# A hybrid decoder layer on one core: the p projection for all tokens in the router, w_in split one step ahead, earlier row norms, later group norms

## The chip, the core and the metric

The kernel runs on one core of one Trainium2 chip. The metric is the device time of one execution in microseconds (us); lower is better. TensorE is called PE, its weight loads PEld, VectorE DVE, ScalarE ACT, GpSimd POOL and SyncE SP. SP only issues DMAs here; POOL issues the indirect ones, and both take their instructions strictly in order.

## The reference, cut to what is computed

One layer over 1024 tokens of width 1024: a Mamba-2 SSD mixer, a mixture of 64 experts (group top-1 of 8 groups, then expert top-2 of 8), and a gated embedding p (1024 x 256) that is projected and added.

```python
h = x + ssd_mixer(rms_norm(x), w_in, conv_w, ..., gnorm, w_out)
h = h + hier_moe(rms_norm(h), w_rg, w_re, w_gate, w_up, w_down)
gate = sigmoid(rms_norm(h) @ ple_w_gate + ple_b_gate)
h = h + gate * (p @ ple_w_proj)            # p: 1024x256, ple_w_proj: 256x1024
return rms_norm(h)
```

The mixer projects u = rms_norm(x) with w_in (1024 x 5152) into z, x, B, C and dt, runs a short convolution, scans 8 chunks of 128 tokens, normalises each of 4 groups of 512 channels and projects back with w_out.

## The kernel before

**SSD.** `ssd` works in two halves of 512 tokens (`hf`) and, in each, four groups (`g`): eight units. A unit's `project` makes ten tiles of 128 output columns: B and C, four of x, four of z. A tile is 24 matmuls (`mm3`, L204 to L206): weights and activations are each split into a high and a low part (`split`, L69 on ACT for wh, L70 on DVE for wl), and three products are summed over 8 blocks of the width. `proj` splits a tile's weights directly ahead of the tile's matmuls. Between the tiles, at step t, `plan` inserts the scan of the unit before (`front`, `back`), and of the unit before that the group norm (`norm`, at t = 0: L394 sums the squares over partitions, then a row of small DVE operations) and its application (`store`, at t = 2: L402 turns it, DVE scales yz, SP stores yn). `x_half(hf)` loads four tiles of x, squares them for the row norms, makes rs (L66), turns it (L177), loads x transposed, scales it and splits it into xh and xl. For the second half it runs inside the fourth unit, at t = 3 to 7. Its x tiles share the buffers "ac" (three) and "ec" (two) with the scan.

**Router.** `out_router` multiplies by w_out in three passes of 2, 3 and 3 token tiles; `route` then yields `first`, `second` and `third`, which for the last pass have no products to run beside (`for f in side: f()`). `first` and `second` are chains of small DVE operations; `third` ranks tokens (L688 and its neighbours on PE), builds one-hot rows (L706 on DVE), packs the token numbers (L714), makes row indices (`index`) and fetches the first group's rows from DRAM (`fetch`, L827); then it packs the gates (L714 again). Meanwhile the first 12 half-tiles (1 MB each) of expert weights are loaded by SP (`half`, L782).

**Experts.** `moe` runs 8 groups of 4 pairs of experts. PE order is written by hand. Each step (`up`, `down`, L1027) uses two halves of 1 MB; a ring of 8 such halves is refilled by SP as PE frees them. The PLE of group g (`ple`) is spread over the steps of group g + 1: turn h (L898), 32 gate products (L908), and per set of rows the projection of p: `turn_p` (2 transposes, L855, ACT copy L856) and `project_p` (4 matmuls of 128x512 over two halves, L861). p rows come by an indirect DMA of 128 rows x 256 (`fetch_p`, L827, after step 10). There are nine such sets: groups 0 to 5 inside groups 1 to 6, groups 6 and 7 early at the end of group 6 (`project`, L1109), and the second row set inside group 7. The tensors' names: w is a raw weight tile, XT the group's tokens turned, py, pup, pgate, pq and pc are PSUM tiles, ha and hb rows of h, uh and ul the two parts of a group's normalised rows, S its selection matrix.

**Order.** On all engines except where PE is ordered by hand, a scheduler sets the order from the program and its own expectations, so the written step numbers move more than their own instructions.

Of the kernel before, what the change touches and what calls it, by code (L numbers as in the profile page):

```python
# [20 lines left out]
KD = D // 128  # L21
# [20 lines left out]
class K:  # L42
# [64 lines left out]
    def ssd(self, left, right):  # L107
# [35 lines left out]
        def x_half(hf):  # L143

            ss, rs, *tmp = (wk.tile([128, HC], F32, name=n) for n in ("rs", "rs", "nt0", "nt1", "nt2"))
            cols = []

            def columns():
                for j in range(2):
                    w = wraw.tile([128, KD, 256], F32, name="w").rearrange("p a b -> p (a b)")  # L150
                    w = w.rearrange("p (k t) -> p k t", t=HT)
                    nc.sync.dma_start(w, a["xT"].rearrange("(k p) t -> p k t", p=128)[:, 4 * j:4 * j + 4,
                                                                                      hf * HT:(hf + 1) * HT])
                    cols.extend(w[:, k] for k in range(4))

            for i in range(HC):
# [3 lines left out]
                if i == HC - 1:  # L160
                    if hf == 0:
                        W.append(load(2 * DI, 2 * DI + 512))
                    columns()
# [14 lines left out]
            rsb = wk.tile([128, HT], F32, name="dT", bufs=1)  # L178
            nc.scalar.activation(rsb, pr.rearrange("p c t -> p (c t)"), AF.Copy)

            def scale(k):
                nc.vector.tensor_mul(cols[k], cols[k], rsb)
# [4 lines left out]
            yield  # L187
# [75 lines left out]
        def proj(w, i, x):  # L263
            wh = wsp.tile([128, KD, 128], F32R, name="wh")
            wl = wsp.tile([128, KD, 128], F32R, name="wl")
            self.split(wh, wl, w[:, :, i * 128:(i + 1) * 128])
            ps = self.ps_mm.tile([128, 512], F32, name="mm")
            mm3(ps, wh, wl, x)
            return ps

        def conv_tile(hf, w, i, x, m):
# [5 lines left out]
            ps = proj(w, i, x)  # L277
# [11 lines left out]
        def project(hf, g):  # L289
            x = X[hf]  # L290
            w = W.pop() if W else load(2 * DI + g * 128, 2 * DI + 512 + g * 128)
            xT, zT = [], zp.tile([128, 4, HT], F32, name="z")
            bT = conv_tile(hf, w, 0, x, 16 + g)
            yield
            cT = conv_tile(hf, w, 1, x, 20 + g)
            U[hf, g] = bT, cT, xT, zT
            yield
            for j in range(2):
                w = load(DI + g * 512 + j * 256)
                for i in range(2):  # L300
                    xT.append(conv_tile(hf, w, i, x, 4 * g + 2 * j + i))
                    yield
            for j in range(2):
                w = load(g * 512 + j * 256)
                for i in range(2):
                    nc.scalar.activation(zT[:, 2 * j + i], proj(w, i, x), AF.Silu)
                    yield
# [104 lines left out]
        X, SZ, U, W = {}, {}, {}, []  # L412
        for i, _ in enumerate(x_half(0)):
            if i == 0:
                nc.sync.dma_start(gk, a["ssd_norm_kp"])
            if i == HC - 1:
                small_loads()
# [3 lines left out]
        for hf, g in units:  # L421
# [35 lines left out]
    def out_router(self, st, tail, after_tail):  # L457
# [18 lines left out]
        self.gdd = dp.tile([128, 8, NE], F32, name="gdd")  # L476
        macc = self.macc
# [82 lines left out]
        for f in side:  # L560
            f()
# [21 lines left out]
    def route(self, t0, hs, rp, pr_p, wr, rb, macc):  # L583
# [95 lines left out]
        def third():  # L679
# [3 lines left out]
            for i in range(n + 1):  # L683
# [5 lines left out]
                if t0:  # L689
                    nc.tensor.matmul(pa[:, i], lhsT=self.onesb, rhs=macc, start=False, stop=True)  # L690
            adj, was = tl("adj", 8)[:, 0], self.more
# [29 lines left out]
            pack(self.mid, omi)  # L721
            started = tc.issue_after(self.index(rp).ins) if t0 + n == T // 128 else nullcontext()
# [16 lines left out]
    def moe_weights(self, st):  # L739
# [3 lines left out]
        wpp = cp.tile([128, 2, D], F32, name="wpp")  # L743
# [4 lines left out]
        self.pl = (wpg, wpp, bg, fn, mgp)  # L748

        def loads():  # L750
# [6 lines left out]
            for k in range(2):  # L757
                nc.sync.dma_start(wpp[:, k], a["ple_w_proj"][k * 128:(k + 1) * 128])
                yield
# [3 lines left out]
            for _ in range(10):  # L763
                yield
# [29 lines left out]
    def moe_buffers(self, st, ring):  # L794
# [4 lines left out]
        self.p0, self.po = (hp.tile([128, PD], F32, name=f"p{i}") for i in range(2))  # L799
# [39 lines left out]
    def fetch_p(self, g):  # L839
        if g < NGR - 1:  # L840
            self.gather(self.p0, self.a["p"], g)
        if self.first_of(g + 1) or g == NGR - 1:
            self.gather(self.po, self.a["p"], NGR + SET[g])
# [8 lines left out]
    def turn_p(self, p, pT, pc_):  # L852
        pt = pc_.tile([128, 2, 128], F32, name="pc")
        for k in range(2):
            self.nc.tensor.transpose(pt[:, k], p[:, k * 128:(k + 1) * 128], self.ident)  # L855
        self.nc.scalar.activation(pT, pt, AF.Copy)  # L856

    def project_p(self, pT, hf, pc_):
        pq = pc_.tile([128, 512], F32, name="pc")
        for k in range(2):  # L860
            self.nc.tensor.matmul(pq, lhsT=pT[:, k], rhs=self.pl[1][:, k, hf * 512:hf * 512 + 512],  # L861
                                  start=(k == 0), stop=(k == 1))
        return pq

    def ple(self, h, p, store, wk, pq_, pc_, own=(), pr=None):
# [3 lines left out]
        wpg, wpp, bg, fn, mgp = self.pl  # L869
# [23 lines left out]
        def tr(k0):  # L893
# [6 lines left out]
            if k0 and pr is None:  # L900
                self.turn_p(p, new("pT", [128, 2, 128]), pc_)
# [26 lines left out]
    def moe(self, s2, ring, sa):  # L928
        nc, tc, a = self.nc, self.tc, self.a
        mgp = self.pl[4]  # L930
# [5 lines left out]
        part = {"vT": vx[:, 0:1024].rearrange("p (k t) -> p k t", k=KD), "gt": vx[:, 1024:1536],  # L936
                "pT": vx[:, 1536:1792].rearrange("p (k t) -> p k t", k=2)}
# [164 lines left out]
        def ple_of(G, i, own=part):  # L1102
# [3 lines left out]
                bounds_check=T - 1, oob_is_err=False), wk, ps1, ps2, own,  # L1106
                            None if i else G.pr)

        def project(p, o):  # L1109

            self.turn_p(p, part["pT"], ps2)
            for hf in range(2):
                nc.scalar.activation(o[:, hf * 512:hf * 512 + 512], self.project_p(part["pT"], hf, ps2), AF.Copy)
                yield

        def ending(G):
# [3 lines left out]
            wpg, wpp, bg, fn, _ = self.pl  # L1120
# [138 lines left out]
        with tc.manual_schedule(engines={mybir.EngineType.PE}):  # L1259
            for g in range(NGR):  # L1260
# [20 lines left out]
                if g == NGR - 2:  # L1281
                    nxt.pr, cur.pr = self.h0[(g + 2) % 3], self.ho[(SET[g] - 1) % 3]
                    fill[2].append(lambda: self.gather(vx[:, 1792:], a["p"], g + 1))
                    early = [project(vx[:, 1792:], nxt.pr), project(self.p0, cur.pr)]
                    for n, x in ((17, 0), (18, 0), (20, 1), (21, 1)):
                        fill.setdefault(n, []).append(lambda x=x: next(early[x]))
# [172 lines left out]
```

## Time and profile before

| | us |
|---|---|
| median of 3 runs | 1950.36 (1946.88 to 1954.07) |
| the profiled execution's own time | 1954.31 |
| its span from the first to the last instruction | 1952.4 |
| SSD stage, about | 0 to 636 |
| w_out and router, about | 636 to 882 |
| experts and PLE, about | 882 to 1952 |

A timeline row gives start, duration, engine, line, output<-input, tile shape and, in brackets, the engine's idle time just before and what ended it. A waits row gives who waited for whom: total us, times, longest. An fp32 matmul (L861, L908) stands in the trace as two records; so the 36 products of L861 are x72.

### The profile page before, as it was taken

How to read it: one execution, taken by the hardware profiler on the slowest of the kernel's cores; microseconds unless marked ns; L12 is line 12 of the kernel's file. 1: busy time of each engine (PE TensorE's matmuls, PEld its weight loads, DVE VectorE, ACT ScalarE, POOL GpSimd, SP SyncE). 2: the span in 40 equal slices, each digit the busy share in tenths (PEclk: the TensorE clock that was granted, in tenths of full speed). 3: DMA queues.
4: the chain of work that ended last, by engine and by line, in shares of the span. 5: the costliest groups of instructions: out<-in, count | busy, mean ns of one | idle time of the engine just before them, and what ended most of it. 6: DMA issues, size and time to landing. Idle time of an engine off the chain costs nothing.

```text
span 1952.4 us, 23158 instructions
## 1 busy us (share of the span) xinstructions
PE 1848.3 (95%) x8702; PEld 1047.1 (54%) x8702; DVE 1031.5 (53%) x2194; ACT 749.5 (38%) x1040; POOL 182.7 (9%) x276
## 2 busy tenths in 40 slices
PE   6999997999999999979999999999999999999996
PEld 4778775777887678863343333433433334334334
DVE  5497896858988876573341514423325244143223
ACT  5476766557767533322021211312222113122223
POOL 1011110201111031021000000000000000000004
PEclk9999998999999999988999999999999999999998
DMA  7425444345442787956999999999999999998883
GB/s 220 118 75 137 115 134 127 88 97 134 110 110 53 243 294 238 346 195 254 422 421 394 401 421 385 412 412 383 420 382 404 420 373 423 404 375 325 337 322 109
DMA packets 192166, 538.39 MB, mean 276 GB/s; under 512 B 16046, under 2 KB 128688, under 8 KB 143920
## 3 DMA queue, kind: packets, MB, share of 16 engines
q1 hardware_dynamic: 177744, 514.21, 72.0%
q10 hardware_dynamic: 11008, 12.94, 2.0%
q0 software_dynamic: 3296, 9.70, 1.3%
q8 instruction: 70, 1.15, 0.2%
q14 instruction: 48, 0.39, 0.1%
HBM read 520.95 MB, written 17.69 MB: 276 GB/s over the span
## 4 chain that ended last, share of the span: by engine, by line
PE 81%; DMA 7%; DVE 7%; ACT 2%; issue 2%; POOL 1%; SPq 0%; POOLq 0%; ACTq 0%; DVEq 0%
PE pup L1027 11%; PE pgate L1027 11%; PE py L1027 10%; PE mm L206 6%; PE mm L204 6%; PE mm L205 6%; PE pq L908 6%; PE pc L1017 3%; PE mm L505 2%; PE mm L506 2%; PE mm L507 2%; DMA w<-in_w_up_dram 2%; PE pc L861 2%; DMA ac<-acd 2%; PE pc L1090 2%
## 5 line engine op out<-in xcount | busy, mean ns | idle before, releaser
L204 PE MATMUL mm<-xh,wh 128*128 128x512 f32 x640 | 265.6, 415 | 3.3 <-ACT xh L197 2.2
L206 PE MATMUL mm<-xh,wl 128*128 128x512 f32 x640 | 254.5, 400 | 8.4 <-DVE wl L70 8.3
L205 PE MATMUL mm<-xl,wh 128*128 128x512 f32 x640 | 253.9, 397 | 0.3 <-DVE xl L198 0.3
L1027 PE MATMUL pup<-w,XT 128*64 128x512 f32 x1016 | 239.1, 598 | 1.6 <-DMA w<-in_w_up_dram 1.6
L1027 PE MATMUL pgate<-w,XT 128*64 128x512 f32 x1000 | 232.7, 599 | 0.0
L1027 PE MATMUL py<-w,hT 128*64 128x512 f32 (+1 forms) x1024 | 227.1, 586 | 2.1 <-DMA w<-in_w_down_dram 2.1
L70 DVE TENSOR_TENSOR yx<-py,yx 128x512 fp32r<-128x512 f32 (+1 forms) x68 | 44.8, 659 | 234.2 <-ACT yx L69 234.2
L1027 PEld LDWEIGHTS py<-w,hT 128*64 128x64 f32 x1024 | 70.0, 137 | 146.2 <-issue 138.2
L1027 PEld LDWEIGHTS pup<-w,XT 128*64 128x64 f32 x1016 | 72.1, 136 | 141.9 <-issue 131.5
L206 PEld LDWEIGHTS mm<-xh,wl 128*128 128x128 f32 x640 | 122.6, 192 | 38.5 <-DVE wl L70 12.2
L204 PEld LDWEIGHTS mm<-xh,wh 128*128 128x128 f32 x640 | 122.9, 192 | 34.2 <-issue 4.5
L1027 PEld LDWEIGHTS pgate<-w,XT 128*64 128x64 f32 x1000 | 68.7, 137 | 134.2 <-issue 129.6
L205 PEld LDWEIGHTS mm<-xl,wh 128*128 128x128 f32 x640 | 123.0, 192 | 29.9 <-issue 4.3
L908 PE MATMUL pq<-wpg,vx 128*128 128x512 f32 x256 | 123.1, 607 | 0.0
L70 DVE TENSOR_TENSOR wl<-w,wh 128x1024 fp32r<-128x1024 f32 x80 | 97.4, 1220 | 46.4 <-ACT wh L69 46.4
L69 ACT ACTIVATE wh<-w 128x1024 fp32r<-128x1024 f32 x80 | 84.3, 1054 | 72.0 <-PE mm L205 59.4
L284 DVE SCALAR_TENSOR_TENSOR xbc<-raw,convw,xbc 128x512 f32<-128x512 f32 x144 | 109.7, 762 | 3.8 <-ACT xbc L282 2.7
L506 PE MATMUL mm<-wl,yh 128*128 128x512 f32 x256 | 99.3, 398 | 2.0 <-DVE wl L517 1.9
L505 PE MATMUL mm<-wh,yh 128*128 128x512 f32 x256 | 96.0, 402 | 4.8 <-ACT yh L69 4.6
L69 ACT ACTIVATE yx<-py 128x512 fp32r<-128x512 f32 (+1 forms) x68 | 38.9, 572 | 159.4 <-PE py L1027 159.4
L1058 ACT ACTIVATE hT<-pt 128x512 f32<-128x512 f32 x31 | 18.4, 593 | 211.5 <-PE pt L1056 211.5
L507 PE MATMUL mm<-wh,yl 128*128 128x512 f32 x256 | 98.0, 393 | 0.0
(360 smaller groups left out, 2815.6 us busy)
## 6 DMA issues: line engine op xcount, KB each, us to landing
w<-in_w_up_dram SPq DMA_DIRECT2D x127, 1024.0 KB, 9.5
w<-in_w_gate_dram SPq DMA_DIRECT2D x125, 1024.0 KB, 9.1
w<-in_w_down_dram SPq DMA_DIRECT2D x120, 1024.0 KB, 9.5
w<-in_w_in_dram SPq DMA_DIRECT2D x32, 1024.0 KB, 5.6
w<-in_w_out_dram SPq DMA_DIRECT2D x48, 512.0 KB, 5.2
ac<-acd SPq DMA_DIRECT2D x32, 512.0 KB, 9.3
w<-in_w_in_dram SPq DMA_DIRECT2D x16, 512.0 KB, 8.7
yn<-yz SPq DMA_DIRECT2D x32, 256.0 KB, 4.4
```

The source lines that it names most:

```text
L69: self.nc.scalar.activation(dst_h, src, AF.Copy)
L70: self.nc.vector.tensor_sub(dst_l, src, r_(dst_h))
L204: nc.tensor.matmul(ps, lhsT=wh[:, k], rhs=x[0][:, k], start=(k == 0), stop=False)
L205: nc.tensor.matmul(ps, lhsT=wh[:, k], rhs=x[1][:, k], start=False, stop=False)
L206: nc.tensor.matmul(ps, lhsT=wl[:, k], rhs=x[0][:, k], start=False, stop=(k == KD - 1))
L284: nc.vector.scalar_tensor_tensor(o, raw[:, j:j + HT], convw[:, m, j:j + 1], o, op0=OP.mult, op1=OP.add)
L505: nc.tensor.matmul(po[i][hf], lhsT=yh[:, ts], rhs=wh[:, cs], start=(k == 0), stop=False)
L506: nc.tensor.matmul(po[i][hf], lhsT=yh[:, ts], rhs=wl[:, cs], start=False, stop=False)
L507: nc.tensor.matmul(po[i][hf], lhsT=yl[:, ts], rhs=wh[:, cs], start=False, stop=(k == 15))
L908: nc.tensor.matmul(V["pq"], lhsT=V["vT"][:, k], rhs=wpg[:, k, cs], start=(k == 0), stop=(k == KD - 1))
L1017: nc.tensor.matmul(px, lhsT=x[:, k], rhs=G.S[:, i], start=(i == 0 and x is u[i][0]), stop=(i == 1 and x is u[i][1]))
L1027: nc.tensor.matmul(ps[64 * b:64 * b + 64], lhsT=xt(k0 + k, b), rhs=w[b][:, k, cs], start=(k0 + k == 0), stop=(k0 + k == K - 1))
```

## The change

1. p arrives transposed (`pT`). `out_router` projects all 1024 tokens: 16 pieces of two matmuls (one piece is 128 tokens x 512 columns), an ACT copy each, and eight stores of 512 KB to a DRAM buffer `ppd`. PE order there is by hand: six pieces after `first`, two after the ranking, two after the first pack, six after `third`. The experts' stage then gathers rows of 1024 instead of 256 from `ppd`; `turn_p`, `project_p` and `project` go; `fetch_p` moves from step 10 to 15; the last group's rows are gathered at step 17 of group 6.
2. `proj` takes a tile's split weights from a generator that runs one tile ahead; the split of the next tile is issued after the current tile's matmuls in program order.
3. `x_half` is cut in two: `norms(hf)` (x tiles, squares, rs, turning into its own tile rsb) and the rest. `norms(1)` runs at t = 2 to 6 of the first unit; `x_half(1)` keeps t = 6 and 7 of the fourth.
4. `norm` and `store` go from t = 0 and 2 to t = 1 and 3.

```diff
-        def proj(w, i, x):
-            wh = wsp.tile([128, KD, 128], F32R, name="wh")
...
+        def proj(x):
+
+            wh, wl = ahead.pop() if ahead else next(W)
             ps = self.ps_mm.tile([128, 512], F32, name="mm")
             mm3(ps, wh, wl, x)
+            ahead.extend(w for w in [next(W, None)] if w)
             return ps
...
+                if hf == 0:
+                    rows = norms(1)
+                    for t in (2, 3, 4, 5, 6):
+                        at(t, next, rows)
             if before:
-                at(0, before[2])
-                at(2, before[3])
+                at(1, before[2])
+                at(3, before[3])
...
             if hf == 0 and g == NG - 1:
                 xg = x_half(1)
-                for t in (3, 4, 5, 6, 7):
+                for t in (6, 7):
                     at(t, next, xg)
...
-        for f in side:
-            f()
+        pT, wpp = [], []
+        for k in range(2):
+            for to, src, name in ((wpp, "ple_w_proj", "w"), (pT, "pT", "wh")):
+                to.append(wp.tile([128, D], F32, name=name, **({"bufs": 3} if name == "w" else {})))
+                nc.sync.dma_start(to[k], a[src][k * 128:(k + 1) * 128])
+        def project():
+
+            for t in range(T // 128):
+                pr = wp.tile([128, D], F32, name="wl")
+                for hf in range(2):
+                    cs = slice(hf * 512, hf * 512 + 512)
+                    pq = self.ps_mm.tile([128, 512], F32, name="mm")
+                    for k in range(2):
+                        nc.tensor.matmul(pq, lhsT=pT[k][:, t * 128:(t + 1) * 128], rhs=wpp[k][:, cs],
+                                         start=(k == 0), stop=(k == 1))
+                    nc.scalar.activation(pr[:, cs], pq, AF.Copy)
+                    if hf:
+                        nc.sync.dma_start(self.ppd[t * 128:(t + 1) * 128], pr)
+                    yield
...
-            self.gather(self.p0, self.a["p"], g)
+            self.gather(self.p0, self.ppd, g)
...
-            nc.vector.tensor_mul(gt, gt, self.project_p(V["pT"], hf, pc_) if pr is None else pr[:, cs])
+            nc.vector.tensor_mul(gt, gt, pr[:, cs])
...
-                    if n == 10:
+                    if n == 15:
                         self.fetch_p(g)
```

**SP, the fourth unit (first half, last group).** Before, the four x tiles of the second half stand here between the scan's loads of acd (the running sums of dt, one 512 KB broadcast per chunk) and w_in's:

```order
L260 DMA w<-in_w_in_dram 128x8x256
L152 DMA w<-in_xT_dram 128x4x512 x2
L159 DMA ac<-in_x_dram 128x1024
L406 DMA yn<-yz 128x4x128 x4
L159 DMA ac<-in_x_dram 128x1024
L322 DMA ac<-acd 128x8x128
L260 DMA w<-in_w_in_dram 128x8x256
L159 DMA ac<-in_x_dram 128x1024
L322 DMA ac<-acd 128x8x128
L260 DMA w<-in_w_in_dram 128x8x128 x2
L159 DMA ec<-in_x_dram 128x1024
L322 DMA ac<-acd 128x8x128 x2
```

After, the same place on SP:

```order
L331 DMA ac<-acd 128x8x128
L258 DMA w<-in_w_in_dram 128x8x256
L331 DMA ac<-acd 128x8x128
L174 DMA w<-in_xT_dram 128x4x512 x2
L331 DMA ac<-acd 128x8x128
L415 DMA yn<-yz 128x4x128 x4
L258 DMA w<-in_w_in_dram 128x8x256
L331 DMA ac<-acd 128x8x128
```

The four x tiles have moved to the first unit, where no scan uses "ac" and "ec" yet; only the two loads of x transposed stay.

**PE, the last pass of the router.** Before, the ranking (L688) follows the router's logits (L618) directly:

```order
L612 MATMUL tp<-ident,h 128x128 x8
L618 MATMUL tp<-wr,uT 128x72 x8
L688 LDWEIGHTS tris
L688 MATMUL tp<-M,tris 128x72
L690 LDWEIGHTS onesb
L690 MATMUL tp<-macc,onesb 128x72
```

After, six pieces (12 matmuls, L592) stand ahead of the ranking (now L735), and the last six between the packing of the gates (L762) and the first spreading of rows in the experts' stage (L1046, before L1017):

```order
L659 MATMUL tp<-ident,h 128x128 x8
L665 MATMUL tp<-wr,uT 128x72 x8
L592 MATMUL mm<-w,wh 128x512 x12
L735 LDWEIGHTS tris
L735 MATMUL tp<-M,tris 128x72
...
L762 MATMUL tp<-oms,at 128x104
L592 MATMUL mm<-w,wh 128x512 x12
L1046 MATMUL pc<-S,uh 128x512 x2
L1046 MATMUL pc<-S,ul 128x512
```

Two and two more pieces stand after the ranking and after the first pack; so all 16 lie ahead of the experts' first matmul.

**SP, the end of the router.** Before, the last three preloaded weight halves (w, yx, vx) follow the ninth:

```order
L513 DMA w<-in_w_out_dram 128x1024 x2
L782 DMA hb_6097<-in_w_gate_dram 128x2048
L782 DMA w<-in_w_gate_dram 128x2048
L782 DMA yx<-in_w_gate_dram 128x2048
L782 DMA vx<-in_w_gate_dram 128x2048
L782 DMA w<-in_w_down_dram 128x2048 x4
```

After:

```order
L532 DMA w<-in_w_out_dram 128x1024 x2
L827 DMA hb_6097<-in_w_gate_dram 128x2048
L583 DMA w<-in_ple_w_proj_dram 128x1024 x2
L583 DMA wh<-in_pT_dram 128x1024 x2
L596 DMA ppd<-wl 128x1024 x8
L827 DMA w<-in_w_gate_dram 128x2048
L827 DMA yx<-in_w_gate_dram 128x2048
L827 DMA vx<-in_w_gate_dram 128x2048
L827 DMA w<-in_w_down_dram 128x2048 x4
```

The three halves, and every load of the ring behind them, now stand behind the eight stores of `ppd`.

## Rows read from the trace of the kernel before

**Rows 1.** The page, busy time by engine and the 40 slices of the span
```profile
PE 1848.3 (95%) x8702; PEld 1047.1 (54%) x8702; DVE 1031.5 (53%) x2194; ACT 749.5 (38%) x1040; POOL 182.7 (9%) x276
...
PEclk9999998999999999988999999999999999999998
DMA  7425444345442787956999999999999999998883
```
**Rows 2.** Waits of PE from 18 to 640 us: total, times, longest
```profile
PE mm L206 <- DVE wl L70: 8.3, 8, 2.2
PE tp L177 <- DVE rs L66: 7.8, 1, 7.8
PE tp L394 <- POOL sqs L389: 4.3, 1, 4.3
PE py L369 <- DVE ac L352: 3.6, 2, 3.5
PE tp L329 <- DVE nt L56: 2.9, 1, 2.9
PE py L369 <- DVE yz L382: 2.7, 1, 2.7
```
**Rows 3.** The chain of waits, start, us, what, around the second half's start
```profile
286.85 10.97 DMA ec<-in_x_dram
...
309.70 9.82 DMA ac<-acd
```
**Rows 4.** Windows of PE: stretch, length, busy (records), granted clock, DMA share, GB/s
```profile
322.00:324.00 2.00, 0.71 (x4) 0.52 0.01 4
324.00:326.00 2.00, 2.00 (x7) 0.50 0.00 0
```
**Rows 5.** Waits of PE from 855 to 890 us
```profile
PE pc L1017 <- ACT uh L1003: 5.6, 2, 4.8
PE tp L688 <- DVE me L664: 4.4, 1, 4.4
PE tp L714 <- DVE at L706: 2.8, 1, 2.8
PE tp L714 <- DVE oms L728: 1.4, 1, 1.4
```
**Rows 6.** A window of PE at the router's end, columns as in Rows 4
```profile
880.00:885.00 5.00, 4.25 (x9) 0.50 0.34 116
```
**Rows 7.** Timeline of SP, issues of the last preloaded half and the ring's first
```profile
859.88 0.43 SPq L782 DMA_DIRECT2D vx<-in_w_gate_dram  x1
...
892.62 9.28 SPq L782 DMA_DIRECT2D w<-in_w_down_dram  x4
```
**Rows 8.** Windows between like places of the groups: PE, PEld, DVE, ACT, POOL, clock, DMA, GB/s
```profile
967.00:1099.00 132.00, 128.94 (x528) 48.83 (x526) 44.05 (x84) 26.96 (x44) 2.02 (x2) 1.00 1.00 403
...
1482.00:1610.60 128.60, 127.35 (x526) 47.38 (x524) 44.04 (x84) 28.28 (x45) 3.04 (x3) 1.00 1.00 403
...
1773.00:1917.00 144.00, 141.09 (x604) 56.59 (x602) 41.09 (x94) 35.46 (x66) 11.07 (x10) 1.00 0.89 328
```
**Rows 9.** Windows of PE inside one group, columns as in Rows 4
```profile
1160.00:1165.00 5.00, 5.00 (x20) 1.00 1.02 424
...
1190.00:1195.00 5.00, 5.00 (x23) 1.00 0.88 315
```
**Rows 10.** Timeline of PE: the work on p in groups 2 and 6
```profile
1149.87 0.38 PE L855 MATMUL pc<-ident,p 128*128 128x128 f32 x2
...
1740.87 2.68 PE L861 MATMUL pc<-wpp,vx 128*128 128x512 f32 x4 [1.96 <-ACT vx L856]
```
**Rows 11.** Chain of waits: eight records of the same shape in a row
```profile
1821.22 3.63 PE pq L908 x8
```
**Rows 12.** Groups by line: L861's records, busy, mean ns, idle before
```profile
L861 PE MATMUL pc<-wpp,vx 128*128 128x512 f32 x72 | 36.3, 627 | 5.0 <-ACT vx L856 2.5 <-DVE ha L1092 1.3 <-DVE hb L1092 1.3
```
**Rows 13.** DMA issues by line: engine, times, median us to landing
```profile
p<-in_p_dram,iall POOLq DMA_INDIRECT x9, 6.0
hb<-hd,iall POOLq DMA_INDIRECT x6, 9.6
```

More of the change, by code (lines that the diff above doesn't have):

```diff
@@ L141, in small_loads, with norms @@
             nc.sync.dma_start(al, bcast_rows(a["a_log"], 128, 0, NH))
-        def x_half(hf):
+        def norms(hf):
             ss, rs, *tmp = (wk.tile([128, HC], F32, name=n) for n in ("rs", "rs", "nt0", "nt1", "nt2"))
[L146 to L154, printed above, removed]
             for i in range(HC):
@@ L410, in scan @@
             return front, back, norm, store
-        X, SZ, U, W = {}, {}, {}, []
-        for i, _ in enumerate(x_half(0)):
+        X, SZ, U, RB = {}, {}, {}, {}
+        first, xg = norms(0), x_half(0)
+        for i in range(HC):
+            next(first)
             if i == 0:
                 nc.sync.dma_start(gk, a["ssd_norm_kp"])
-            if i == HC - 1:
-                small_loads()
+        ahead.append(next(W))
+        next(xg)
+        small_loads()
+        next(first)
+        next(xg)
         sizes = step_sizes(0)
@@ L476, in out_router @@
         self.gdd = dp.tile([128, 8, NE], F32, name="gdd")
+        self.ppd = dp.tile([T, D], F32, name="ppd")
         macc = self.macc
@@ L559, in out_router @@
             side += rest
-        for f in side:
-            f()
+        pT, wpp = [], []
[6 more added lines that the diff above has]
+                pr = wp.tile([128, D], F32, name="wl")
+                for hf in range(2):
+                    cs = slice(hf * 512, hf * 512 + 512)
[6 more added lines that the diff above has]
+                        nc.sync.dma_start(self.ppd[t * 128:(t + 1) * 128], pr)
+                    yield
+        pieces = project()
+        with tc.manual_schedule(engines={mybir.EngineType.PE}):
+            for f in side[:-3]:
+                f()
+            for n, f in zip((6, 0, 0), side[-3:]):
+                f() if f is not side[-1] else f(lambda n: [next(pieces, None) for _ in range(n)])
+                for _ in range(n):
+                    next(pieces)
+            for _ in pieces:
+                pass
         for _ in extra:
@@ L762, in loads @@
             nc.sync.dma_start(fn, bcast_rows(a["final_norm"], 128, 0, D))
-            for _ in range(10):
+            for _ in range(12):
                 yield
@@ L798, in moe_buffers @@
         self.h0, self.ho = ([hp.tile([128, D], F32, name=f"ha{i}"), b[:, 0], b[:, 1]] for i, b in enumerate(self.spare))
-        self.p0, self.po = (hp.tile([128, PD], F32, name=f"p{i}") for i in range(2))
+        self.p0, self.po = (hp.tile([128, D], F32, name=f"p{i}") for i in range(2))
         self.iall = hp.tile([128, NGR + NSET], I32, name="iall")
@@ L840, in fetch_p @@
         if g < NGR - 1:
-            self.gather(self.p0, self.a["p"], g)
+            self.gather(self.p0, self.ppd, g)
         if self.first_of(g + 1) or g == NGR - 1:
-            self.gather(self.po, self.a["p"], NGR + SET[g])
+            self.gather(self.po, self.ppd, NGR + SET[g])
     def parts(self, to, v, k, w):
@@ L850, in parts, with ple @@
         mm(to, lhsT=v[1][:, k], rhs=w[0], start=False, stop=(k == KD - 1))
[L852 to L865, printed above, removed]
+    def ple(self, h, pr, store, wk, pq_, pc_, own=()):
         nc = self.nc
-        wpg, wpp, bg, fn, mgp = self.pl
+        wpg, bg, fn, mgp = self.pl
         V = dict(own)
@@ L1105, in ple_of @@
                 out=self.out, out_offset=self.rows(n), in_=v, in_offset=None,
[L1106 to L1114, printed above, removed]
+                bounds_check=T - 1, oob_is_err=False), wk, ps1, ps2, own)
         def ending(G):
             h, D4 = G.hg[0], D // 4
-            wpg, wpp, bg, fn, _ = self.pl
+            wpg, bg, fn, _ = self.pl
             o = G.pr
@@ L1281, in moe @@
                 if g == NGR - 2:
[L1282 to L1286, printed above, removed]
+                    nxt.pr = self.h0[(g + 2) % 3]
+                    fill.setdefault(17, []).append(lambda: self.gather(nxt.pr, self.ppd, g + 1))
                 if nxt:
```

86 lines of the change are left out of this document (46 added, 40 removed).

## The prediction

> **What bounds the kernel now.** I read the page first: PE is busy 1848.3 of 1952.4 us, no other engine more than 53%, and the DMA engines' share is near nine tenths from the 17th slice on [rows 1]. So PE's time is the span but for its gaps, and in the experts' stage the DMA is a close second. Then I went through PE's waits stage by stage, because a mean over three stages says nothing on any of them.
>
> In the SSD stage PE's gaps are few and each has a name. Eight short ones end with the low part of a weight split (8.3 us in all), one of 7.8 us with the second half's row norms, one of 4.3 us with the squares for a group norm, one of 2.9 us with the group norm's first DVE operation; the scan's own are 3.6 and 2.7 us [rows 2]. The chain shows why the row norms are late: the fourth x tile needs 10.97 us from issue to landing in the middle of the scan's traffic, and a load of acd behind it needs 9.82 us more [rows 3]. A gap also costs the clock: after the waits at 312 to 322 us PE works at a granted clock of 0.50 to 0.52, its 1.2 GHz level, where 2.7 us of busy time do the work of half of that [rows 4].
>
> At the router's end PE waits 5.6 + 4.4 + 2.8 + 1.4 = 14.2 us for DVE chains and the first rows [rows 5], and afterwards works at 0.50 [rows 6]. The DMA queue is idle there: SP issues the last preloaded half at 859.88 us and the next load at 892.62 [rows 7].
>
> In the experts' stage the five periods of groups 1 to 5, 967 to 1610.6 us (the first and the last of five stand in the rows), have PE busy 98 to 99% and a DMA share of 1.00 at 403 GB/s [rows 8]. That share is no proof of a full feed: in a group's light steps it delivers 424 GB/s, in its heavy ones, where PE frees ring buffers more slowly, 315 [rows 9]. From 1773 us on its share is 0.89 [rows 8].
>
> **p in the router: what it removes.** An fp32 product of this shape takes two records, and eight records in a row take 3.63 us [rows 11], so 0.454 us each. The 72 records of L861 are 32.7 us. The transposes take 0.38 us a set [rows 10], 3.4 us for nine. PE idles 5.0 us ahead of L861, for the ACT copy and for PSUM buffers that DVE must release [rows 12]; the early sets at 1740 us show it at its largest, 1.96 us of idle time and 2.68 us for four records that take 1.8 elsewhere [rows 10]. Together 41.1 us, 4.57 a set.
>
> How much of it ends up in the span depends on the weights.
> Groups 1 to 5 hold five sets. If PE alone set their time, 643.6 us would become 643.6 - 22.8 = 620.8. The DMA moved 643.6 us x 403 GB/s = 259.4 MB there; the gathers of p grow from 128 to 512 KB, 0.39 MB each, so 261.3 MB, which at 424 GB/s, the best rate in the rows, need 616 us. The two limits lie within 5 us of each other, and the ring of four pairs evens out only part of the light and heavy steps. I take 15 us of the 22.8; the ends are 0 and 23.
> Groups 6 and 7 hold the other four sets, 18.3 us. There the DMA has room (0.89), so PE's time counts: I take 17, with ends 10 and 20.
> Group 0 only loses. Two gathers of p, 0.8 MB more, now fall into its time, and the last three preloaded halves stand on SP behind the eight stores of ppd instead of leaving at 859.88. They are 3.1 MB, 7.5 us of transfer, needed some 20 us after the stage's start. I take +2, with ends 0 and 9.
>
> **What it adds.** Sixteen pieces are 32 products, 64 records, 29.0 us. They fill the 14.2 us of waits: six pieces stand ahead of the ranking, where PE waited 4.4 us, so the ranking comes 6 to 7 us later, and two times two pieces cover 2.8 and 1.4 us. The last six run while the first rows are fetched (5.6 us). As PE then goes from the logits to the experts without a pause, its spreading of rows need not run at 0.50; 8 us of work at half the clock around 880 to 888 give back 4. Sum 29.0 - 14.2 - 4 = +11. The ends: 9, if the clock gives back more, and 17, if it gives back nothing and pT, which must wait for the buffer of the last w_out products, comes 2 us after them. ACT's sixteen copies and the stores lie beside PE. Behind the stores on SP wait the three halves and the ring, priced above; behind the p gather on POOL, which must wait for all eight stores, waits only the next group's fetch of h, needed a period later.
>
> **The split one step ahead.** It adds nothing but order: the next tile's split runs beside the current tile's 24 products. The eight waits for wl, 8.3 us, should go. The price is that DVE and ACT reach the scan's operations later.
>
> **Row norms and group norms.** The row norms' 7.8 us go: their four x tiles, squares and 13 small DVE operations move to the first unit, where no scan runs; four transposes move with them. On SP the x tiles now pass between loads of w_in; this costs 2 MB of transfer in a stage whose DMA share is about 0.4 to 0.7 [rows 1]. The group norm one step later should take away the 4.3 and the 2.9 us. Named waits: 8.3 + 7.8 + 4.3 + 2.9 = 23.3. The clock gives back some 1.35 us for each of up to five restarts like that of [rows 4], so at most 30. What is late next: the loads of acd, 9.82 us [rows 3], with the scan's waits of 3.6 and 2.7; and at the half's start xh can only be written when the last z tile is done. I take 20, with 30 and, as only the row norms' wait has no successor in the trace, 8 as ends.
>
> **Sum.** -20 + 11 - 15 - 17 + 2 = -39 us. Against the profiled execution's 1954.3 that is 1915.3; the median of the runs is 3.9 lower than that execution, so 1911.
>
> **The rivals.**
> *The weight feed binds.* For it: share 1.00 in all five periods. Against: the dips to 315 GB/s while PE does not wait. Then groups 1 to 5 gain nothing and pay 5 x 0.39 MB at 403 GB/s, +5: -20 + 11 + 5 - 17 + 2 = -19, 1931. The Trainium skill, in DMA: Bandwidth & Descriptors (Specifications), puts a core's HBM limit at about 358 GB/s; by it this rival would be certain. The rows have 403 over whole periods and 424 at best, so the measurement decides against that figure.
> *All of it counts.* Every term at its good end: -30 + 9 - 23 - 20 = -64, 1886. For it: PE is 95% busy. Against: the DMA limit just worked out.
> *The SSD stage does not do what it says.* The other waits move up and only the 7.8 us stay won: -8 + 11 - 15 - 17 + 2 = -27, 1923. With the bound feed as well, -7: 1943.
> *Slower: the larger gathers hold the DMA engines.* A gather of 512 KB lands after 9.6 us, one of 128 KB after 6.0 [rows 13]. If the engines lose the whole 3.6 us in a stage with share 1.00, ten gathers cost 36, groups 1 to 5 gain nothing: -20 + 11 - 17 + 2 + 36 = +12, 1962. It decides from 24 / 10 = 2.4 us a gather; its bytes alone are 0.9 us. The same page of the Trainium skill (Queues, rings and completion order) says that each DMA engine takes turns between queues packet by packet, which would leave a gather the price of its bytes; no row here shows the turns.
>
> **How the numbers follow.** Forecast 0.50 (1900 to 1922), bound feed 0.20, SSD stage as it was 0.10, all of it 0.08, the two together 0.06, slower gathers 0.06. A measurement of this kernel tells about 0.5%, 10 us, from no change: faster 0.88, same 0.06 (1943), slower 0.06. All ends together would reach from 1886 to 1958; the range 1892 to 1937 leaves out the two last cases and most of "all of it", under 2 in 10.
>
> **What would show it.** Right: no wait of PE for rs of the second half, waits for wl under 2 us; PE without a gap from the logits to the first spreading, at a clock of 1.00, and the experts' first gate products some 11 us later relative to the logits; periods of groups 1 to 5 of 124 to 126 us at over 410 GB/s; group 6 shorter by some 15 us. Wrong: periods that stay at 127 to 129 with waits for w in them (feed), new waits of PE for ac or xh at the half's start (SSD), a wait for w at the fifth step of group 0 (the late halves).

## The result, and the profile after

The changed kernel takes 1921.03 us, the median of four runs (1915.14 to 1924.22); the kernel before took 1950.2 on the same chips. The ratio is 0.9846, 95% interval 0.9816 to 0.9876: 1.5% faster. Forecast were 1911 and a range of 1892 to 1937. The direction, the range and most of the sum held; the gain is 29 us instead of 39.

The profiled execution took 1920.88 us. The page of the changed kernel, the lines that answer to [rows 1]:

```profile
PE 1832.3 (95%) x8676; PEld 1045.4 (54%) x8676; DVE 1033.7 (54%) x2194; ACT 758.7 (40%) x1047; POOL 186.3 (10%) x276
...
PEclk9999999999999999999999999999999999999998
DMA  8334454354434786948999999999999999999892
```

PE lost 16 us of busy time and 17 us of gaps. The clock's digits are nines up to the last slice; the dips of [rows 1], in the 7th slice (the second half's start) and in the 18th and 19th (the router's end), are gone at this resolution.

This table sets the stages of both kernels side by side, and of all experiments, so that each term of the sum has its row. Its marks are starts in PE's timeline: the last product with w_in, the last router logits, the first gate product of the experts, the first spreading of rows (L1017, L1046) of groups 1 and 6, and the end of the span. One profiled execution stands behind the times of each row. Kernels with the same SSD code have their last logits at 842 to 848 us (e4 alone at 838), so a difference of 3 us in that column tells nothing.

Most of that spread is PE's clock. Added up over 10 us windows from 30 us to the logits, the time in which PE was granted a clock of 0.50 is 14 us in e4, 20 in e8 and e9, 24 in the changed kernel and e11, 27 in e7 and e12 and 31 in e6, and the logits come nearly in that order: 838, then 842 and 843, 843 and 844, 845 and 845, 848. The kernel before has 34 us, 10 more than the changed one; as half of such time is lost, I estimate that some 5 of the 19 us between the two are the clock's.

| kernel | ratio to before, 95% | last w_in | last logits | to 1st gate product | group 0 | groups 1-5 | 6-7 |
|---|---|---|---|---|---|---|---|
| before | 1 | 633.4 | 862.4 | 24.3 | 102.7 | 639.6 | 323.4 |
| changed | 0.9846 (0.9816-0.9876) | 608.2 | 843.1 | 37.1 | 101.8 | 629.0 | 307.9 |
| e1 no split ahead | 0.9921 (0.9896-0.9945) | 630.6 | 861.9 | 38.1 | 102.5 | 626.9 | 306.1 |
| e2 late norms | 0.9871 (0.9846-0.9897) | 611.0 | 846.8 | 37.8 | 102.0 | 624.6 | 305.8 |
| e3 old group norm | 0.9836 (0.9812-0.9861) | 607.3 | 846.7 | 38.9 | 101.9 | 627.9 | 306.6 |
| e4 SSD parts only | 0.9895 (0.9871-0.9920) | 603.5 | 837.7 | 23.7 | 102.1 | 639.8 | 321.9 |
| e5 split only | 0.9953 (0.9940-0.9967) | 616.8 | 851.1 | 24.3 | 102.7 | 640.4 | 323.4 |
| e6 less feed | 0.9758 (0.9739-0.9778) | 610.2 | 848.2 | 37.5 | 99.3 | 617.2 | 303.4 |
| e7 small gather | 0.9787 (0.9771-0.9804) | 607.7 | 845.3 | 37.6 | 101.9 | 622.5 | 304.9 |
| e8 rounded p | 0.9819 (0.9796-0.9842) | 604.6 | 842.4 | 31.4 | 102.5 | 629.6 | 305.7 |
| e9 even PLE | 0.9759 (0.9736-0.9782) | 608.0 | 843.4 | 39.5 | 101.9 | 617.4 | 302.0 |
| e10 split first | 0.9846 (0.9824-0.9867) | 615.3 | 847.7 | 37.4 | 101.9 | 626.3 | 306.0 |
| e11 even PLE, late gather | 0.9762 (0.9744-0.9780) | 609.9 | 844.0 | 37.5 | 102.0 | 617.2 | 302.6 |
| e12 e11 and e8 | 0.9717 (0.9700-0.9733) | 609.6 | 845.3 | 31.4 | 101.9 | 617.2 | 302.1 |

Waits of PE in the changed kernel's SSD stage, 18 to 608.7 us (who waited for whom: total, times, longest), against [rows 2]:

```profile
PE mm L204 <- DVE wl L70: 6.7, 7, 2.2
PE mm L202 <- ACT xh L195: 5.6, 2, 3.5
PE mm L202 <- ACT wh L69: 2.0, 1, 2.0
PE tp L338 <- DVE cbm L345: 1.9, 1, 1.9
PE tp L338 <- DVE nt L56: 1.7, 2, 0.9
```

The waits for rs of the second half, for sqs and those of py for ac and yz are gone, as hoped. But seven of the eight waits for wl are still there, and a new one for xh of 3.5 us stands at the second half's start. And yet the last w_in product comes 25 us earlier. That contradiction is what the first five experiments are about.

At the router's end, 843 to 884 us, against [rows 5]:

```profile
PE pc L1046 <- DVE ul L1033: 1.2, 1, 1.2
PE pc L1046 <- DVE S L999: 1.0, 1, 1.0
PE mm L592 <- ACT wl L594: 0.4, 1, 0.4
```

14.2 us of waits have become 2.6. The products of p themselves, PE's timeline of the changed kernel (start, duration, and at the end the number of records):

```profile
844.98 10.51 PE L592 MATMUL mm<-w,wh 128*128 128x512 f32 x24
...
855.75 3.68 PE L592 MATMUL mm<-w,wh 128*128 128x512 f32 x8
...
859.41 3.68 PE L592 MATMUL mm<-w,wh 128*128 128x512 f32 x8
...
863.21 8.81 PE L592 MATMUL mm<-w,wh 128*128 128x512 f32 x20
872.41 1.98 PE L592 MATMUL mm<-w,wh 128*128 128x512 f32 x4 [0.39 <-ACT wl L594]
```

That is 28.7 us, and a window over them shows the clock at 1.00 (columns as in [rows 8]; [rows 6] had 0.50):

```profile
843.00:880.00 37.00, 34.39 (x119) 16.48 (x117) 17.89 (x68) 15.08 (x27) 7.20 (x17) 1.00 0.48 172
```

In the experts' stage, groups 1 to 5 as a whole, from the first spreading of group 1's rows to that of group 6's (columns as in [rows 8]); first the kernel before, then the changed one:

```profile
989.40:1629.00 639.60, 633.72 (x2611) 237.15 (x2611) 220.21 (x421) 141.37 (x225) 15.53 (x15) 1.00 1.00 402
...
982.10:1611.00 628.90, 617.63 (x2560) 234.25 (x2560) 220.58 (x421) 139.47 (x220) 15.11 (x15) 1.00 1.01 412
```

The stage is shorter and the rate is up from 402 to 412 GB/s, but PE idles longer than before: 11.3 us in it, where the kernel before had 5.9.

### The profile page after: what moved, and what is told of

Read it like the earlier page. It is cut to its first block, busy times and chain, and to the rows that moved or that the text cites. A ratio compares the mean times of both kernels' runs of the same rounds, so it can differ in the third digit from the quotient of the medians.

```text
span 1919.0 us, 23163 instructions
## 1 busy us (share of the span) xinstructions
PE 1832.3 (95%) x8676; PEld 1045.4 (54%) x8676; DVE 1033.7 (54%) x2194; ACT 758.7 (40%) x1047; POOL 186.3 (10%) x276
## 5 line engine op out<-in xcount | busy, mean ns | idle before, releaser
L1056 PE MATMUL pup<-w,XT 128*64 128x512 f32 x1016 | 243.3, 598 | 4.6 <-DMA w<-in_w_up_dram 4.6
L1056 PEld LDWEIGHTS pup<-w,XT 128*64 128x64 f32 x1016 | 77.3, 136 | 141.0 <-issue 120.3
L1056 PEld LDWEIGHTS py<-w,hT 128*64 128x64 f32 x1024 | 72.2, 136 | 145.9 <-issue 134.6
L202 PEld LDWEIGHTS mm<-xh,wh 128*128 128x128 f32 x640 | 122.5, 191 | 38.1 <-ACT xh L195 6.2
## 6 DMA issues: line engine op xcount, KB each, us to landing
w<-in_w_down_dram SPq DMA_DIRECT2D x120, 1024.0 KB, 10.6
```

Source lines behind the costliest of these rows:

```text
L202: nc.tensor.matmul(ps, lhsT=wh[:, k], rhs=x[0][:, k], start=(k == 0), stop=False)
L1056: nc.tensor.matmul(ps[64 * b:64 * b + 64], lhsT=xt(k0 + k, b), rhs=w[b][:, k, cs], start=(k0 + k == 0), stop=(k0 + k == K - 1))
```

## The experiments

**Theory and rival for the SSD stage.** Theory A is the prediction: each named wait goes with its part of the change. Theory B: the waits' names say little, and one part carries nearly all. Three kernels undo one part each, two do one side alone.

**e1, the split directly ahead of its tile again:**

```diff
             mm3(ps, wh, wl, x)
-            ahead.extend(w for w in [next(W, None)] if w)
             return ps
```

> The changed kernel without part 2: a tile's weights are split directly ahead of its own matmuls again; row norms early, group norm late and p in the router stay. Theory A (the prediction: each named wait goes with its part): the waits for wl of 8.3 us come back, so the last router logits end at about 851 us instead of 843 and the run takes about 1929 us. Theory B (the split one step ahead brings nothing, because the changed kernel still shows seven waits for wl, 6.7 us): logits at 842 to 845, run 1920 to 1923.

Both expectations fell, A the less: the logits end at 861.9 us, 19 later, and the run takes 1937.5. Nearly the whole gain of the SSD stage goes. Its waits, 18 to 640 us, first rows:

```profile
PE mm L202 <- ACT wh L69: 6.6, 2, 4.9
PE mm L204 <- DVE wl L70: 4.2, 5, 2.2
PE mm L202 <- ACT xh L195: 4.0, 2, 2.2
PE py L377 <- DVE yz L390: 3.6, 3, 1.4
PE py L377 <- DVE ac L360: 3.5, 1, 3.5
```

The waits for wl are not larger but smaller than in the changed kernel. The scan's waits for yz and ac are back, and those for wh are larger than in either kernel (2.0 in the changed one, 1.2 before). The reason can be read in PE's timeline of the kernel before, around the longest wait of the second unit, with DVE's split of the same tile below:

```profile
96.23 0.48 PE L204 MATMUL mm<-xh,wh 128*128 128x512 f32 x1
96.55 0.40 PE L205 MATMUL mm<-xl,wh 128*128 128x512 f32 x1
100.43 1.12 PE L369 MATMUL py<-ac,xc 128*64 128x128 f32 x6 [3.48 <-DVE ac L352]
101.84 0.80 PE L206 MATMUL mm<-xh,wl 128*128 128x512 f32 x1 [0.29 <-DVE wl L70]
102.43 0.63 PE L204 MATMUL mm<-xh,wh 128*128 128x512 f32 x1
...
100.56 1.22 DVE L70 TENSOR_TENSOR wl<-w,wh 128x1024 fp32r<-128x1024 f32 x1
```

After two products the tile needs its wl, which DVE begins only at 100.56. As I read it, the scheduler therefore put the scan's py next; PE stood 3.48 us for ac with 22 products of the tile undone, then went on at a granted clock of 0.50 (a product every 0.43 us). In the changed kernel wl is there, the tile runs on at 1.00 (one every 0.23 us), and py comes behind it, without a wait:

```profile
99.04 0.48 PE L202 MATMUL mm<-xh,wh 128*128 128x512 f32 x1
99.35 0.39 PE L203 MATMUL mm<-xl,wh 128*128 128x512 f32 x1
99.58 0.40 PE L204 MATMUL mm<-xh,wl 128*128 128x512 f32 x1
...
104.37 0.39 PE L204 MATMUL mm<-xh,wl 128*128 128x512 f32 x1
104.68 1.09 PE L378 MATMUL py<-ac,xc 128*64 128x128 f32 x16
```

The wait named "ac" was the price of the late split: it is gone with the split ahead alone (e5), and back with 3.5 us in e1. The generator also loads a tile's weights earlier, but that is not what pays: in the kernel before, the changed one, e1 and e5 no split of the SSD stage is shown waiting for a load of w_in.

**e2, the row norms back in the fourth unit:**

```diff
-                if hf == 0:
-                    rows = norms(1)
-                    for t in (2, 3, 4, 5, 6):
-                        at(t, next, rows)
...
                 xg = x_half(1)
+                rows = norms(1)
+                for t in (3, 4, 5, 6, 7):
+                    at(t, next, rows)
```

> The changed kernel with the second half's row norms moved back into the fourth unit (steps 3 to 7), all else kept. Theory A: the 7.8 us wait for rs comes back and with it one or two stretches at half clock (1.35 to 4 us); logits at 852 to 855, run 1930 to 1933. Theory B (the row norms carry nearly the whole 19 us of the SSD and w_out stages, the other two parts nothing): logits at 858 to 862, run 1936 to 1940.

Both fell: the logits end at 846.8, 3.7 later, and the two intervals overlap. No wait for the second half's rs is back; instead wl takes 8.6 us. The fourth unit is 6.5 us longer than in the changed kernel (table below).

**e3, the group norm at its old steps:**

```diff
-                at(1, before[2])
-                at(3, before[3])
+                at(0, before[2])
+                at(2, before[3])
```

> The changed kernel with norm and store back at t = 0 and 2. Theory A: the waits for sqs (4.3) and nt (2.9 us) come back: logits at about 850, run about 1928. Theory B (those waits were a consequence of the late row norms and not of the step): logits at 842 to 845, run 1920 to 1923, no wait for sqs over 1.5 us.

Theory B holds for the run, though not for the logits: 1921.96 against 1921.03, no loss that can be measured, and no wait for sqs over 0.9 us. The waits for nt are larger by some 3.5 us, but the stage to the last w_in product is 1 us shorter; the logits end 3.5 us later, behind a wait for yh of 7.7 us in the w_out stage and with 31 us at the half clock instead of 24; neither shows in the run's time. The 4.3 and 2.9 us of [rows 2] did not hang on these steps alone.

**e4, parts 2 to 4 in the kernel before, p as it was.**

> The kernel before with parts 2 to 4 (split ahead, early row norms, later group norm); p is projected in the experts' stage as before. Theory A (the parts add): logits at 843, then the router's and the experts' stages as before (periods of groups 1 to 5 of 127 to 131 us): 13 us less for the router and 27 us more for the experts than the changed kernel, so about 1935 us. Rival (the earlier start of the experts changes their feed, so that p's part is worth more or less than 14 us): 1928 or less, or 1941 or more.

1931.1 us. The router's and the experts' stages are those of the kernel before, so part 1 is what tells e4 from the changed kernel there: 13.4 us more for the router and 25.1 less for the experts. The logits end 5 us earlier than in the changed kernel though the SSD code is the same. That is the clock: 14 us at 0.50 up to there against 24, some 5 us of work; between 300 and 410 us alone the mean is 0.97 against 0.94. Why it fell less often here, these traces don't tell.

**e5, part 2 alone in the kernel before.**

> The kernel before with part 2 alone (the split one step ahead). Theory A (the order of the splits is by itself worth most of what the SSD stage won, since without it the changed kernel loses 15 us): second unit 73 to 75 us instead of 80.6, fourth unit 79 to 81 instead of 85.4, last router logits at 846 to 851 us instead of 862, run about 1938. Rival (the split ahead pays only together with the early row norms and the later group norm): logits at 856 or later, run 1945 or more.

Between the two: the logits end at 851.1, as theory A had it by its far end, but the run is only 9 us faster (0.9953, 0.9940 to 0.9967). The second unit takes 73.3 us. So the split ahead is worth 9 us alone, and 15 us when it is the part taken away (e1): the rest of the gain needs it. The eight units, from the last w_in product of one to that of the next, the first from its first product (us):

```
unit              1     2     3     4     5     6     7     8
before         64.5  80.6  70.4  85.4  91.1  80.3  71.5  71.9
changed        65.4  73.9  72.1  72.3  89.3  76.5  70.4  70.6
e1 no split    66.4  79.2  72.2  75.0  87.7  83.4  74.4  74.6
e2 late norms  65.2  72.9  72.2  78.8  86.1  77.4  70.1  70.6
e5 split only  65.6  73.3  71.2  82.7  85.8  79.0  69.7  71.8
```

The split makes the second unit's gain (6.7 us) and part of the sixth's; of the fourth's 13 us the early row norms make 6.5 by e2. The fifth unit, the half's start, stays at 86 to 91 us in all of them.

**e10, the next split marked urgent.** Could the seven waits for wl be had as well?

```diff
-                            self.split(wh, wl, w[:, :, i * 128:(i + 1) * 128])
+                            with tc.high_priority():
+                                self.split(wh, wl, w[:, :, i * 128:(i + 1) * 128])
```

> The changed kernel with the split of the next tile's weights marked as urgent for the scheduler, so that ACT and DVE take it ahead of scan work that is ready at the same time. Theory A (the seven waits for wl that the changed kernel keeps, 6.7 us, come from the place that the scheduler gave the split in DVE's row, behind instructions that wait themselves): waits for wl under 2 us, last router logits at 834 to 839 us, run about 1913. Rival (the scan's operations are then late instead): logits at 842 or later, other waits of TensorE larger by what wl's lose.

The rival: the ratio is 0.9846 again, and the waits only change names. 18 to 845 us:

```profile
PE tp L339 <- DVE nt L56: 5.2, 3, 1.8
PE tp L412 <- DVE rs L66: 4.5, 1, 4.5
PE mm L525 <- ACT yh L69: 4.5, 1, 4.5
...
PE mm L204 <- DVE wl L70: 2.9, 4, 0.9
```

**Theory and rival for the experts' stage.** Groups 1 to 5 won 10.6 us of the 22.8 that PE no longer works or waits for. Theory F: PE now waits for weights. Rival P: new waits for PSUM hold it. Both are in the waits of the changed kernel, 982 to 1611 us:

```profile
PE pc L1119 <- DVE hb L1121: 3.4, 4, 0.8
PE pup L1056 <- DMA w<-in_w_up_dram: 3.2, 4, 1.0
PE pc L1046 <- DVE hb L1121: 1.9, 3, 0.6
...
PE py L1056 <- DMA w<-in_w_down_dram: 0.8, 1, 0.8
```

The combination (L1119) takes the PSUM tiles that the projection of p had stood between, and waits for DVE to release them: a wait that took the place of the one removed.

**e6, 2 of 48 MB of weights less in each group:**

The steps whose load is left out multiply by the half loaded before, so the output is not the layer's.

```diff
-                w = [self.half(wd, e + b, k0, 2) for b in range(2)]
+                if k0 == 0 or j != 2:
+                    B["w"] = [self.half(wd, e + b, k0, 2) for b in range(2)]
+                w = B["w"]
```

> The changed kernel in which each group's third pair loads only the first half of its w_down (2 of 48 MB a group less), and multiplies by that half twice; TensorE's work is unchanged, the output differs. Theory F (what groups 1 to 5 did not win, some 10 of 23 us, is time in which TensorE waits for weights, openly or inside its matmuls at the fourth to sixth step of a group): no wait for w in groups 1 to 5 and from the first spreading of group 1's rows to that of group 6's 615 to 620 us instead of 629 (627 in the mean of the runs with this experts' stage). Rival P (the new waits for the PSUM tiles of the combination, <- hb and ha, hold it): 625 to 629 us, waits for hb and ha unchanged.

Theory F. The waits that are left, 985 to 1604 us, are those of rival P alone, and they are as large as in the changed kernel:

```profile
PE pc L1121 <- DVE hb L1123: 3.3, 4, 0.8
PE pc L1046 <- DVE hb L1123: 2.6, 4, 0.7
PE pc L1046 <- DVE ha L1123: 1.3, 2, 0.7
PE pc L1121 <- DVE ha L1123: 0.8, 1, 0.8
```

Groups 1 to 5 take 617.2 us, 22.4 less than before, nearly the 22.8 that were promised. The same PE work as in the changed kernel's row for these groups, columns as in [rows 8]:

```profile
985.00:1602.20 617.20, 609.72 (x2561) 227.81 (x2561) 220.38 (x421) 139.58 (x220) 15.10 (x15) 1.00 1.00 403
```

Note the busy time: 617.6 against 609.7 us for 2560 records. With the 4.0 us of named waits for w this makes up the 11.7 us between the two. So I read the 8 us as waiting for weights that stands inside the matmuls' own time, where PE's list of waits does not name it.

The weight loads bear this out. PEld's waits in the changed kernel, 982 to 1611 us:

```profile
PEld pup L1056 <- DMA w<-in_w_up_dram: 7.7, 7, 1.9
...
PEld py L1056 <- DMA w<-in_w_down_dram: 1.8, 2, 1.7
```

These 9.5 us are named for w where PE's own list has 4.0. In e6 PEld has no such wait, in the kernel before 3.5 us. And the 8 us of busy time lie where these waits are: in e6 the products into pup take 145.9 us instead of 152.4 and those into py 144.8 instead of 146.2, those into pgate 146.2 in both. One of the waits, at the end of a group, as PE and as PEld show it:

```profile
1221.52 3.65 PE L1056 MATMUL pup<-w,XT 128*64 128x512 f32 x14 [0.62 <-DMA w<-in_w_up_dram]
...
1221.51 0.20 PEld L1056 LDWEIGHTS pup<-w,XT 128*64 128x64 f32 x4 [1.50 <-DMA w<-in_w_up_dram]
```

That e6 comes out so near the 22.8 is in part chance: it has none of the 3.5 us that the kernel before waited for w, but 8.0 us of waits for PSUM where that kernel had 5.3. So rival P is not nothing either.

**e7, gathers of p of 128 instead of 512 KB:**

```diff
-            self.gather(self.p0, self.ppd, g)
+            self.gather(self.p0[:, 0:256], self.ppd, g)
```

> The changed kernel in which the gathers of p rows for groups 0 to 6 fetch 256 of the 1024 columns (128 instead of 512 KB, as before the change), the rest of the row set keeping old values; the output differs. If the feed binds, 0.39 MB a gather at 410 GB/s are 0.95 us each, some 5 us over groups 1 to 5 (622 instead of 627); if a gather of 512 KB blocks the DMA engines for longer than its bytes, 10 us or more; if the feed does not bind, 0 to 1 us.

The rest of the row set keeps old values, so the output is not the layer's. The first case: 622.5 us, 4.9 less than the 627.4 that six kernels with this experts' stage (changed, e1, e2, e3, e8, e10) take on the mean, or 0.98 us a gather, about the price of its bytes. As the six lie between 624.6 and 629.6, it could be 0.4 to 1.4. The forecast's rival of slower gathers needed 2.4 us each. The whole run gained more than this stage shows, 0.9787 against 0.9846 or some 11 us for seven gathers; where the rest of it lies stays open.

**e9 and e11, the PLE spread over the group:**

```diff
-                          else ((2, 3, 4, 5, 6, 7, 8, 9, 10, 11, 12, 13),))
+                          else ((2, 3, 5, 7, 9, 11, 12, 14, 15, 17, 18, 20),))
...
-                    if n == 15:
+                    if n == 20:
                         self.fetch_p(g)
```

> The changed kernel with the pieces of a group's PLE (turning h, 32 gate products, the additions) spread over steps 2 to 20 of the next group instead of 2 to 13, and the gather of p rows behind the last of them (step 20). The work is the same. Theory F (TensorE waits for weights because the light steps of a group use them up faster than they come, while the mean of 415 GB/s would do): groups 1 to 5 take 618 to 622 us instead of 627, nearly no wait for w, run about 1912. Rival (the mean rate is the bound, at whatever steps the work stands): 626 to 630 us, run 1920 to 1923.

> As e9, and the gather of the last group's p rows, which in e9 still stood at step 17 of group 6 and overwrote rows of h that the spread-out PLE of group 5 was reading, moved to step 21. Theory F: the time of e9 holds, 1903 to 1908, groups 1 to 5 at 617 to 619 us. Rival (e9's gain came in part from the early gather): 1910 or more.

e9 still gathers the last group's rows into rows of h that the spread-out PLE reads, so its output is not the layer's; e11 gathers them four steps later and computes the layer. Theory F again: 617.4 and 617.2 us for groups 1 to 5, as in e6, but now with all weights loaded, and 1906.5 us for e11. Its windows line:

```profile
983.50:1600.60 617.10, 611.76 (x2560) 232.12 (x2560) 225.41 (x421) 138.19 (x219) 14.05 (x14) 1.00 1.01 420
```

420 GB/s over five groups. The feed could deliver what PE needs on the mean; what it could not do was follow light and heavy steps. But not all of e11's gain is the feed's: its waits for PSUM are 4.2 us instead of 7.3, as the combination (L1119) no longer waits, so some 3 of the 11.8 us are rival P's. e6's and e11's equal times are made up differently. e6 has 8.0 us of waits for PSUM and none for w; e11 has these 4.2 and, by PEld, 2.9 for w. What is left in both is PE's own work, some 609 to 610 us.

**e8, p projected in single short products:**

```diff
-            for to, src, name in ((wpp, "ple_w_proj", "w"), (pT, "pT", "wh")):
-                to.append(wp.tile([128, D], F32, name=name, **({"bufs": 3} if name == "w" else {})))
-                nc.sync.dma_start(to[k], a[src][k * 128:(k + 1) * 128])
+            for to, src, name in ((wpp, "ple_w_proj", "wl"), (pT, "pT", "wh")):
+                raw = wp.tile([128, D], F32, name="w", bufs=3)
+                nc.sync.dma_start(raw, a[src][k * 128:(k + 1) * 128])
+                to.append(wp.tile([128, D], F32R, name=name))
+                nc.scalar.activation(to[k], raw, AF.Copy)
...
-                pr = wp.tile([128, D], F32, name="wl")
+                pr = wp.tile([128, D], F32, name="w", bufs=3)
```

> The changed kernel with p and its weights rounded once on ScalarE to the matmul's fast fp32 form, so that each of the 32 products takes one short record of about 0.23 us in place of two of 0.45 us: 7.3 us of TensorE instead of 28.7. Theory A (at the router's end the products lie on the path beyond the 14 us of waits that they cover): from the last logits to the experts' first gate products 24 to 28 us instead of 37, run about 1911. Rival (the ranking chains or the stores of ppd set the end, so that fewer products only bring the waits back): 34 us or more, run 1918 or more.

Neither: 31.4 us from the logits to the first gate product, 6 less than the changed kernel, though the products' records sum to 10.8 us instead of 28.7. The run's ratio is 0.9819; its interval overlaps that of the changed kernel. PE's longest wait there, 843 to 890 us:

```profile
PE pc L1048 <- DVE S L1001: 8.0, 1, 8.0
```

and those of DVE:

```profile
DVE slot L984 <- ACT uh L1034: 7.3, 1, 7.3
DVE S L1001 <- DMA ppd<-w: 2.4, 1, 2.4
```

DVE has slot's numbers ready at 855.9 us but waits before it writes slot and S. The second wait is for a store of ppd, which S does not read. The first is named for uh, which stood behind the fetch of the first rows; in e12 the same wait, 7.65 us, is named for a store. In the kernel before slot follows its input without a wait; in the changed kernel it waits for the last products of p (843 to 880 us):

```profile
DVE slot L982 <- PE mm L592: 8.7, 1, 8.7
```

In the program, slot and S lie in a pool that is opened when the router's pools have just been closed. So I take it that they are written where p's rows and weights stood, and that the work on p sets when the experts' tiles can be written; I infer this from these rows and did not run a kernel with other memory for them. The pause also costs the clock: PE is granted 0.66 from 850 to 860 us and 0.50 from 865 to 874, where the changed kernel has 1.00, and goes from the first spreading to the first gate product in 6.4 us instead of 4.9.

**e12, e11 and e8 together.**

> e11 and e8 together: the PLE spread over steps 2 to 20 and p projected in single short products. If the two gains lie in different stages and add (14 us in the experts, 6 us at the router's end): 1897 to 1903. Rival (an earlier start of the experts only makes them wait for weights): 1904 or more, with waits for w in group 0.

1897.45 us (five runs, 1897.07 to 1901.06), ratio 0.9717 (0.9700 to 0.9733): the two gains add, and this is the fastest of the kernels here. p and its weights are rounded once to the fast fp32 form there.

## Why the prediction was right, and where it was not

**SSD, -20.** By the logits -19 in the profiled execution, some -18 by the mean of seven kernels with this SSD code (844.5, without e4), and -20 by the runs of e4, which has these parts alone (0.9895). The size was right and the shares were wrong, so that they add up to it is luck. The step that failed is the sum of named waits, 8.3 for the split, 7.8 for the row norms, 7.2 for the group norm. The runs gave 15 us (e1) or 9 (e5) to the split, 5 or less to the row norms (e2), nothing measurable to the group norm (e3); in these shares stands what the clock gave back, some 5 us in all by the estimate above. Waits for wl should have come under 2 us and are 6.7; the scan's, which I kept as "late next", went. What I had listed as late next at the half's start did come: xh, 3.5 us. The end of -8, "only the 7.8 us stay won", rested on the wrong wait.

**Router, +11.** It measured +13 (24.3 to 37.1 us; 14 on the mean). The products took 28.7 us (29.0 forecast), the clock stayed at 1.00 as forecast. Mis-sized was the cover: 11.6 of the 14.2 us of waits went, 2.6 stayed, for S and the first low parts.

**Group 0, +2.** It measured -0.9; the three late halves (w_gate) were issued at 876.6 to 879.6 us and no product into pgate waits for them.

**Groups 1 to 5, -15 of a possible 22.8.** -10.6, and -12.5 by the means (639.9 of three kernels with the old stage, 627.4 of six with the new). The reason given, a feed limit near PE's, is what e6, e7 and e11 show. Too high was the share that I let the ring save: "evens out only part of the light and heavy steps" held, but a smaller part than taken; PEld's waits for w rose from 3.5 to 9.5 us. That the combination would wait for PSUM (4.2 us) I did not see. The 643.6 us of the sum were read from windows not cut at like places: the first of [rows 8] is 132 us, where the spreadings lie 127.1 apart. By the spreadings the five periods took 639.6, which hardly changes the term.

**Groups 6 and 7, -17.** -15.5, and -16.5 by the means.

**Sum.** -19 + 13 - 1 - 11 - 16 = -34 against -39, so 1920 of 1954; the median says 29.

**Readings.** DMA's digits in [rows 1] are 5 and 6 in the 18th and 19th slice, so near nine tenths only from the 20th on, and 2 to 7 in the SSD stage; no term hangs on it.

**Rivals.** The bound feed is half true: bound behind the light steps at a group's end, where PEld's waits stand, not on the mean, and so at -10.6 and not at +5. Slower gathers fell by e7.

## What to carry to other kernels

A wait's name tells which operand came last, not which order made it late: before a wait is summed, ask what the engine would have done had its other work been ready. Undo each part once; the sum of several parts can be right with every share wrong. And where two limits lie within 1% of each other, spread the heavy work evenly before taking work away: e11's new row of steps gave some 16 us at no cost in work.

## What the runs showed of the hardware

The DMA share reads 1.00 or 1.01 at 402, 403, 412 and 420 GB/s alike (before, e6, changed, e11), so it does not tell how far the feed is from its best. And waiting for a weight can stand in a trace as matmul time: 8 us of "busy" in five groups went with 4% of the bytes (e6), and 6 in e11 with all of them. PEld's list of waits showed it better than PE's, 9.5 us against 4.0.
